# Self-attention exponentials turned by VectorE and DMAs instead of TensorE, with heads scored in pairs

## Chip, cores and metric

One of the eight cores of a Trainium2 chip runs the whole program. The metric is the device time of one execution, in microseconds; the kernel before takes 2255.77 us (median of three runs).

## The reference

A trunk of two layers is applied with the same weights to a prompt of 1024 rows and a sample of 256 rows, 1024 wide. Each layer adds to x the normalised projection of four groups of heads (attention, fourier, spatial gating, memory attention). Only the attention group is touched:

```python
q = apply_axial_rope(rms_norm(aq, q_g), cos, sin)      # 8 heads of 64
k = apply_axial_rope(rms_norm(ak, k_g), cos, sin)      # 2 heads of 64
s = jnp.einsum('bqkgd,bskd->bkgqs', qblk, k) * scale   # blocks of 128 queries
p = jax.nn.softmax(s, axis=-1)
o_att = jnp.einsum('bkgqs,bskd->bqkgd', p, v) * silu(ag)
```

The prompt's queries see 1024 keys, the sample's 256. All is in float32.

## The kernel before

The program is written as Python generators on top of a layer that assigns buffers and semaphores. Within a layer it runs the spatial gating, fourier and memory groups, then `attention_qkv` (keys, values and queries), `attention_gates`, `attention` and `output`. From the second step of `attention` on, the order of TensorE's instructions is the order in which they are written; on the other engines and on SP, which issues every DMA, the layer's scheduler sets the order.

`attention` walks over ten tiles of 128 queries (eight of the prompt, two of the sample), and in a tile over eight heads. Three stages are interleaved:

- `score` (L742): the head's scores, two matmuls of 512 keys for each half of a float32 product (the queries hold a high and a low part in rows 0 to 63 and 64 to 127, the keys' two parts are `kT[..][0]` and `kT[..][1]`), into a two-bank PSUM tile of the tag `s2` (two buffers). VectorE takes the row maximum (L755), ScalarE the exponentials and their sum (L757).
- `turn` (L760): the 128x1024 exponentials are transposed on TensorE in eight 128x128 pieces (L770) and copied out of PSUM by ScalarE (L773) and VectorE (L775), into a buffer `pt` with the keys on the partitions.
- `norm_gate` and `values` (L777, L788): while the next tile is scored, the last tile's `pt` is multiplied with the values, one block of 128 keys per head step, the two key heads into the upper and lower 64 rows of one PSUM bank; the result is multiplied with the gate over the row sum (L801) and stored (L803).

One step of the loop is written as: score of the next head, a step of the last tile's values, turn of this head. In tile 0 the last products of `attention_gates` are interleaved (L1012), in tiles 8 and 9 a product of `output` per head (L1014).

The tag `a16` has four buffers, which hold the layer's input `hT` until the gates are done and `pt` afterwards; `a8` has two, which hold the third group of `hT` until the last gate product.

Of the kernel before, what the change touches and what calls it, by code (L numbers as in the profile page):

```python
# [9 lines left out]
F32 = mybir.dt.float32  # L10
# [5 lines left out]
P = 128  # L16
# [58 lines left out]
def trunk_kernel(  # L75
# [93 lines left out]

# [1 line left out]
    slabs = []  # L171
# [26 lines left out]

# [1 line left out]
    def norm_begin(x_sb):  # L200
# [74 lines left out]

# [1 line left out]
    mk_d = [dram(f"mk{l}", [P, 4, 512]) for l in range(DEPTH)]  # L277
# [56 lines left out]

# [1 line left out]
    def sgu_pair(l, hT, i, o_d, wsT, bsp, vg, between=lambda: None):  # L336
# [43 lines left out]

# [1 line left out]
    def fourier_setup(l):  # L382
# [19 lines left out]
    def fourier_group(l, hT, h, o_d, cw, pos):  # L402
# [135 lines left out]

# [1 line left out]
    def memory_setup(l):  # L540
# [77 lines left out]

# [1 line left out]
    def attention_gates(l, hT, ag):  # L620
# [90 lines left out]

    def attention(l, q_d, kT, v8, v2, ag, o_d):
        def prep_q(t):
            q = c2([P, 8, HD])
            nc.sync.dma_start(q, q_d[t])
            qhl = c4([P, 8, 2, HD], F32R)
            split(qhl[:, :, 0, :], qhl[:, :, 1, :], q)
            return qhl

        def turn_q(qhl, qT, kvs):  # L720
            for kv in kvs:
                pt = mm([P, 4, P], F32R)
                for j in range(4):
                    nc.tensor.transpose(pt[:, j, :], qhl[:, 4 * kv + j].rearrange("p a d -> p (a d)"), ident_r)
                if kv == 0:
                    nc.scalar.copy(qT[:, 0:4], fv(pt))  # L726
                else:
                    nc.vector.tensor_copy(qT[:, 4:8], fv(pt))

        tiles = {}  # L730

        def open_tile(t):
            g, _ = group_of(t)
            nk = SEQ if g < 2 else DEC
            gt = c2([P, 4, P])
            nc.sync.dma_start(gt, ag[t])
            alloc = a16 if g < 2 else c4
            tiles[t].update(
                nk=nk, gt=gt, rs=st([P, 4, 2], tag="rowsum", bufs=3),
                pt=[alloc([P, nk // P, 4, P], F32) for _ in range(2)])  # L740

        def score(t, h):  # L742
            g, _ = group_of(t)
            e = tiles[t]
            nk = e["nk"]
            kv, j = h // 4, h % 4
            s = s2([P, 1024])
            for kg in ((0, 1) if g < 2 else (2,)):
                n = GROUPS[kg][1]
                c0 = GROUPS[kg][0] if g < 2 else 0  # L750
                for b in range(2):
                    nc.tensor.matmul(s[:, c0:c0 + n], e["qT"][:, h, :], kT[kg][b][:, kv, :],  # L752
                                     start=b == 0, stop=b == 1)
            nm = st([P, 1])
            nc.vector.tensor_reduce(nm, s[:, :nk], axis=AX.X, op=ALU.max, negate=True)  # L755
            p = c4([P, 1024])
            nc.scalar.activation(p[:, :nk], s[:, :nk], AF.Exp, bias=nm, accum_out=e["rs"][:, j, kv:kv + 1])  # L757
            e[h] = p

        def turn(t, h):  # L760
            e = tiles[t]
            nkt = e["nk"] // P
            kv, j = h // 4, h % 4
            p = e.pop(h)
            for half in range((nkt + 3) // 4):
                kn = min(4, nkt)
                pt = mm([P, 4, P])
                for kk in range(kn):
                    c0 = (half * 4 + kk) * P
                    nc.tensor.transpose(pt[:, kk, :], p[:, c0:c0 + P], ident)  # L770
                dst = e["pt"][kv][:, half * 4:half * 4 + kn, j, :]
                if half == 0:
                    nc.scalar.copy(dst, pt[:, :kn])  # L773
                else:
                    nc.vector.tensor_copy(dst, pt[:, :kn])  # L775

        def norm_gate(t):  # L777
            e = tiles[t]
            r = st([P, 4, 2], tag="rowsum_r", bufs=2)
            nc.vector.reciprocal(r, e["rs"])  # L780
            rb = c2([P, 4, 2, HD])
            nc.vector.tensor_copy(rb, r.unsqueeze(3).to_broadcast([P, 4, 2, HD]))
            rt = mm([P, 4, P])
            for j in range(4):
# [3 lines left out]
        def values(t, kt):  # L788
            e = tiles[t]
            nkt = e["nk"] // P  # L790
            if kt == 0:
                e["acc"] = mm([P, 4, P])
            acc = e["acc"]
            for kv in range(2):
                vt = (v8 if t < 8 else v2)[:, kt, kv * HD:(kv + 1) * HD]
                nc.tensor.matmul(acc[kv * HD:(kv + 1) * HD].rearrange("p j t -> p (j t)"), vt,  # L796
                                 e["pt"][kv][:, kt].rearrange("p j t -> p (j t)"),
                                 start=kt == 0, stop=kt == nkt - 1)
            if kt == nkt - 1:
                o = c2([P, 4, P])  # L800
                nc.vector.tensor_tensor(o, acc, e["gt"], ALU.mult)  # L801
                for j in range(4):
                    nc.sync.dma_start(o_d[j][:, t * P:(t + 1) * P], o[:, j, :])  # L803
                del tiles[t]

        qhl = prep_q(0)
        yield
        tiles[0] = dict(qT=c4([P, 8, P], F32R))
        turn_q(qhl, tiles[0]["qT"], (0, 1))
        open_tile(0)  # L810
        score(0, 0)
        yield
        work = [(t, h) for t in range(NT) for h in range(8)]
        todo = []
        for i, (t, h) in enumerate(work):
            if h == 2 and t + 1 < NT:
                qhl = prep_q(t + 1)
            if h == 4 and t + 1 < NT:
                tiles[t + 1] = dict(qT=c4([P, 8, P], F32R))
                open_tile(t + 1)  # L820
            if i + 1 < len(work):
                score(*work[i + 1])
            if todo:
                todo.pop(0)()
            if h in (4, 5) and t + 1 < NT:
                turn_q(qhl, tiles[t + 1]["qT"], (h - 4,))
            turn(t, h)
            if h == 7:
                for f in todo:
                    f()  # L830
                todo = [lambda t=t: norm_gate(t)]
                nkt = tiles[t]["nk"] // P
                todo += [lambda t=t, kt=kt: values(t, kt) for kt in range(nkt)]
                if nkt == 8:
                    a, b = todo[0], todo[1]
                    todo[0:2] = [lambda a=a, b=b: (a(), b())]
            yield t, h
        for f in todo:
            f()
        yield NT, 0  # L840

# [1 line left out]
    def rows_of(arr, t):  # L843
# [100 lines left out]

# [1 line left out]
    xin = [rows_of((x_prompt, x_sample), t) for t in range(NT)]  # L946
# [23 lines left out]
    for l in range(DEPTH):  # L970
# [136 lines left out]
```

## Time and profile before

| | us |
|---|---|
| median of three runs (2255.02 to 2256.5) | 2255.77 |
| span of the profiled execution | 2254.6 |
| TensorE busy in it | 2208.9 |
| VectorE busy | 1167.4 |
| ScalarE busy | 844.2 |
| GpSimd busy | 206.3 |

The page gives the profiled execution's span, from its first to its last instruction, and no time beside it; the span lies 1.2 us under the median of the runs. Busy matmul time is modelled, and two matmuls in the pipeline overlap, so a step's length is read from the distance of starts and not from the busy time.

### The profile page before, as it was taken

The numbers are of one execution on the slowest core, as the hardware profiler recorded it, in microseconds if no ns is written. First come the engines' busy times: TensorE is split into PE (matmuls) and PEld (weight loads), VectorE is DVE, ScalarE is ACT, GpSimd is POOL, SyncE is SP. The second block draws the span as 40 slices with busy tenths as digits, with TensorE's granted clock in tenths as the row PEclk, the third lists the DMA queues.
The fourth block names the chain that finished last, engine by engine and source line by source line (L and its number), as shares of the span: only waits on it lengthen the run. The fifth ranks groups of instructions, "written<-read, shape, count | busy, mean of one in ns | idle before, by whom it ended". The sixth has DMA issues, their size and how long they took to land.

```text
span 2254.6 us, 32607 instructions
## 1 busy us (share of the span) xinstructions
PE 2208.9 (98%) x12872; PEld 1837.5 (82%) x12872; DVE 1167.4 (52%) x2096; ACT 844.2 (37%) x1915; POOL 206.3 (9%) x376
## 2 busy tenths in 40 slices
PE   7999999999999999999999999999999999999997
PEld 7898988888998655578888988888899865567885
DVE  5345344545573777634465344445467377753445
ACT  6133332334332655541254222234342255554121
POOL 2010000000140000000062000000014000000005
PEclk9999999999999999999999999999999999999998
DMA  4123321201122210222343121020112221123234
GB/s 171 59 96 132 128 93 59 99 31 55 58 76 75 66 34 29 84 80 92 112 142 109 57 75 59 33 99 31 59 54 81 78 64 29 31 83 99 88 109 140
DMA packets 96200, 177.31 MB, mean 79 GB/s; under 512 B 12208, under 2 KB 47408, under 8 KB 96048
## 3 DMA queue, kind: packets, MB, share of 16 engines
q1 hardware_dynamic: 96048, 175.23, 23.1%
q8 instruction: 101, 1.65, 0.3%
q14 instruction: 51, 0.42, 0.1%
HBM read 129.05 MB, written 46.14 MB: 78 GB/s over the span
## 4 chain that ended last, share of the span: by engine, by line
PE 90%; ACT 2%; DMA 2%; DVE 2%; POOL 2%; issue 1%; SPq 0%; DVEq 0%; POOLq 0%; ACTq 0%
PE mm L248 34%; PE mm L877 16%; PE mm L261 12%; PE mm L796 6%; PE mm L770 6%; PE s L752 5%; PE mm L311 2%; PE mm L327 1%; PE s L422 1%; PE s L408 1%; PE s L576 1%; PE mm L609 1%; POOL c L902 1%; PE s L217 1%; DMA wr<-in_w_in_dram 1%
## 5 line engine op out<-in xcount | busy, mean ns | idle before, releaser
L248 PE MATMUL mm<-a,ws 128*128 128x512 f32 (+1 forms) x4032 | 795.4, 355 | 0.0
L248 PEld LDWEIGHTS mm<-a,ws 128*128 128x128 f32 x4032 | 663.9, 189 | 102.3 <-issue 0.5
L877 PE MATMUL mm<-ws,a 128*128 128x512 f32 x1632 | 380.5, 391 | 0.0
L877 PEld LDWEIGHTS mm<-ws,a 128*128 128x128 f32 x1632 | 303.9, 188 | 63.7 <-issue 1.6
L261 PE MATMUL mm<-ws,a 128*128 128x256 f32 x2400 | 302.7, 287 | 0.0
L261 PEld LDWEIGHTS mm<-ws,a 128*128 128x128 f32 x2400 | 295.6, 194 | 0.5 <-DVE a L234 0.2
L757 ACT ACTIVATE c<-s,st 128x1024 f32<-128x1024 f32 (+1 forms) x160 | 158.1, 988 | 154.8 <-DVE st L755 153.9
L755 DVE TENSOR_REDUCE st<-s 128x1 f32<-128x1024 f32 (+1 forms) x160 | 170.2, 1064 | 73.1 <-PE s L752 71.0
L770 PEld LDWEIGHTS mm<-ident,c 128*128 128x128 f32 x1088 | 117.1, 141 | 90.1 <-issue 26.0
L273 ACT ACTIVATE c<-mm 128x512 f32<-128x512 f32 (+1 forms) x96 | 50.7, 528 | 342.1 <-PE mm L248 338.3
L274 DVE SCALAR_TENSOR_TENSOR c<-c,mm 128x512 f32<-128x512 f32 (+1 forms) x96 | 57.3, 597 | 231.3 <-ACT c L273 231.3
L752 PE MATMUL s<-c,c 128*128 128x512 f32 (+1 forms) x576 | 162.6, 399 | 1.1 <-ACT c L726 1.1
L770 PE MATMUL mm<-ident,c 128*128 128x128 f32 x1088 | 151.8, 279 | 5.0 <-ACT c L757 5.0
L796 PE MATMUL mm<-a,c 128*64 128x512 f32 x512 | 140.2, 618 | 2.7 <-ACT a L773 2.7
L902 POOL TENSOR_TENSOR c<-c,c 128x512 f32<-128x512 f32 x40 | 56.1, 1401 | 891.5 <-ACT c L897 891.4
L166 ACT ACTIVATE ws<-wr,pre_g 128x256 fp32r<-128x256 f32 x304 | 126.6, 505 | 22.6 <-DMA wr<-in_w_in_dram 16.5
L167 DVE SCALAR_TENSOR_TENSOR ws<-wr,pre_g,ws 128x256 fp32r<-128x256 f32 x304 | 128.7, 484 | 2.2 <-ACT ws L166 2.0
L886 DVE TENSOR_TENSOR c<-c,mm 128x512 f32<-128x512 f32 x120 | 81.1, 682 | 85.1 <-PE mm L877 85.1
L775 DVE COPY a<-mm 128x512 f32<-128x512 f32 x128 | 88.3, 690 | 66.3 <-PE mm L770 66.1
L752 PEld LDWEIGHTS s<-c,c 128*128 128x128 f32 x576 | 98.5, 189 | 14.9 <-ACT c L726 1.3
L150 POOL TENSOR_TENSOR st<-st,mhalf 128x1 f32<-128x1 f32 (+3 forms) x120 | 99.7, 831 | 9.9
L148 POOL TENSOR_SCALAR st<-st 128x1 f32<-128x1 f32 (+3 forms) x120 | 27.2, 227 | 744.2 <-DVE st L654 455.5
(119 smaller groups left out, 2133.9 us busy)
## 6 DMA issues: line engine op xcount, KB each, us to landing
wr<-in_w_in_dram SPq DMA_DIRECT2D x76, 512.0 KB, 4.0
wr<-in_w_out_dram SPq DMA_DIRECT2D x32, 512.0 KB, 4.5
wr<-o SPq DMA_DIRECT2D x64, 256.0 KB, 2.9
c<-in_x_prompt_dram SPq DMA_DIRECT2D x16, 512.0 KB, 6.1
o<-c SPq DMA_DIRECT2D x32, 256.0 KB, 2.0
wr<-in_w_mem_kv_dram SPq DMA_DIRECT2D x16, 512.0 KB, 4.4
q<-c SPq DMA_DIRECT2D x40, 128.0 KB, 1.7
ag<-c SPq DMA_DIRECT2D x80, 64.0 KB, 1.6
```

The source lines that it names most:

```text
L150: nc.gpsimd.tensor_tensor(r, m, mhalf[:, :n], ALU.pow)
L166: nc.scalar.activation(w[:, 0, kk], raw[:, k], AF.Copy, scale=g)
L167: nc.vector.scalar_tensor_tensor(w[:, 1, kk], raw[:, k], g, fv(w)[:, 0, kk], ALU.mult, ALU.subtract)
L248: nc.tensor.matmul(acc[:, :n], w[:, a, k, c * P:(c + 1) * P], hT.t[g][b][:, k, :], start=i == 0, stop=i == 3 * KC - 1)
L261: nc.tensor.matmul(acc[:, :256], hT.t[g][a][:, k, tt * P:(tt + 1) * P], w[:, b, k, :], start=i == 0, stop=i == 3 * KC - 1)
L752: nc.tensor.matmul(s[:, c0:c0 + n], e["qT"][:, h, :], kT[kg][b][:, kv, :], start=b == 0, stop=b == 1)
L755: nc.vector.tensor_reduce(nm, s[:, :nk], axis=AX.X, op=ALU.max, negate=True)
L757: nc.scalar.activation(p[:, :nk], s[:, :nk], AF.Exp, bias=nm, accum_out=e["rs"][:, j, kv:kv + 1])
L770: nc.tensor.transpose(pt[:, kk, :], p[:, c0:c0 + P], ident)
L775: nc.vector.tensor_copy(dst, pt[:, :kn])
L796: nc.tensor.matmul(acc[kv * HD:(kv + 1) * HD].rearrange("p j t -> p (j t)"), vt, e["pt"][kv][:, kt].rearrange("p j t -> p (j t)"), start=k ...
L877: nc.tensor.matmul(acc, oT[g][c][:, a, tt * P:(tt + 1) * P], w[:, b, c, :], start=j == 0, stop=j == 11)
```

## The change

Heads are scored in pairs (a unit is a tile, a half of its heads and a key head; four units make a tile). The high part of the keys is multiplied as before. Of the low part, which needs 64 rows only, the first head of a pair uses rows 0 to 63 of the array and the second rows 64 to 127; `prep_q` lays the parts of odd heads the other way round for that. The exponentials no longer go to TensorE: VectorE transposes them in 32x32 blocks into a buffer `d` of the tag `a8` (1 MB per unit), one DMA stores `d` to DRAM, and four DMAs read it back, each into 32 partitions of `pt`. The values of a half tile are written two units after its second unit, in 256-column matmuls. The subtraction of the queries' low part and the spread of 1/sum go from VectorE to GpSimd. `output` is stepped twice per unit.

```diff
         def prep_q(t):
...
-            split(qhl[:, :, 0, :], qhl[:, :, 1, :], q)
+            for odd in range(2):
+                hi, lo = qhl[:, odd::2, odd, :], qhl[:, odd::2, 1 - odd, :]
+                nc.scalar.copy(hi, q[:, odd::2])
+                nc.gpsimd.tensor_tensor(lo, q[:, odd::2], fv(hi), ALU.subtract)
...
+        def open_half(t, hf):
+            e = tiles[t]
+            gt = c2([P, 2, P])
+            nc.sync.dma_start(gt, ag[t][:, 2 * hf:2 * hf + 2])
+            e[hf] = dict(gt=gt, rs=st([P, 2, 2], tag="rowsum", bufs=4), pt=a16([P, 2, 2 * e["nk"]], F32))
...
-            s = s2([P, 1024])
-            for kg in ((0, 1) if g < 2 else (2,)):
...
+            for s, h in zip(ss, hs):
+                for kg in kgs:
+                    nc.tensor.matmul(s[:, cols(kg)], e["qT"][:, h, :], kT[kg][0][:, kv, :], start=True, stop=False)
+            for kg in kgs:
+                for i, (s, h) in enumerate(zip(ss, hs)):
+                    r = slice(64 * i, 64 * i + 64)
+                    nc.tensor.matmul(s[:, cols(kg)], e["qT"][r, h, :], kT[kg][1][r, kv, :], start=False, stop=True)
...
-                    nc.tensor.transpose(pt[:, kk, :], p[:, c0:c0 + P], ident)
...
+            d = a8([P, 2 * nk], F32)
+            dv = d.rearrange("p (b k j q) -> p b k j q", b=4, j=2, q=32)
+            for j, p in enumerate(e.pop((hf, kv))):
+                nc.vector.transpose(dv[:, :, :, j].rearrange("p b k q -> p k b q"),
+                                    p[:, :nk].rearrange("p (k b q) -> p k b q", b=4, q=32))
+            n = nk // 2
+            far = dram(uid(f"turned{l}_"), [4, 32, 4, n])
+            nc.sync.dma_start(far.rearrange("a i b f -> (a i) (b f)"), d)
+            pt = e[hf]["pt"][:, kv].rearrange("p (a f) -> p a f", a=4)
+            for b in range(4):
+                nc.sync.dma_start(pt[32 * b:32 * b + 32], far[:, :, b].rearrange("a i f -> i a f"))
...
+            nc.gpsimd.tensor_copy(rb, r.unsqueeze(3).to_broadcast([P, 2, 2, HD]))
...
+                pt = e["pt"][:, kv].rearrange("p (a k f) -> p a k f", a=4, k=nkt)[:, :, kt]
+                nc.tensor.matmul(acc[kv * HD:(kv + 1) * HD].rearrange("p a j q -> p a (j q)"), vt, pt,
...
+        units = [(t, hf, kv) for t in range(NT) for hf in range(2) for kv in range(2)]
...
+        lag = 3
+        for i, (t, hf, kv) in enumerate(units):
...
+            if i + 1 < len(units):
+                if kv == 1:
+                    open_half(*units[i + 1][:2])
+                score(*units[i + 1])
...
+            turn(t, hf, kv)
+            if i >= lag and (i - lag) % 2 == 0:
...
+                todo.append([lambda u=(tt, hh): norm_gate(*u)] + steps[:nkt // 2])
+                todo.append(steps[nkt // 2:])
...
                 if t >= 8:
                     next(out)
+                    next(out)
```

How it moves instructions, at three places. On SP before, between two tiles of the prompt (`ag` and `q` are loads of gates and queries, `o` the stores of a tile's result):

```order
L715 DMA c_1109_7911<-q_4_5916 128x512
L736 DMA c_1122_7963<-ag_4_6769 128x512
L803 DMA o_0_177<-c_1092_7836 128x128
L803 DMA o_1_178<-c_1092_7836 128x128
L803 DMA o_2_179<-c_1092_7836 128x128
L803 DMA o_3_180<-c_1092_7836 128x128
L715 DMA c_1163_8135<-q_5_5917 128x512
```

On SP now, over some two units (L782 is the store of `d`, L785 x4 its four reads into `pt`, here a):

```order
L785 DMA a_1185_8103<-turned_1208_8182 32x4x512 x4
L782 DMA turned_1220_8225<-a_1219_8222 128x2048
L782 DMA turned_1234_8276<-a_1233_8273 128x2048
L741 DMA c_1236_8294<-ag_6_6771 128x256
L785 DMA a_1185_8103<-turned_1220_8225 32x4x512 x4
L815 DMA o_2_179<-c_1235_8290 128x128
L815 DMA o_3_180<-c_1235_8290 128x128
L785 DMA a_1212_8203<-turned_1234_8276 32x4x512 x4
L782 DMA turned_1247_8325<-a_1246_8322 128x2048
```

Where a whole tile had six DMAs, each unit now adds a store and four reads, and the store of the next unit can stand ahead of the reads of this one. On VectorE, at the start of the first layer's attention (L766 is the row maximum, L274 a gate product's last step, L778 the block transposes into `d`):

```order
L274 SCALAR_TENSOR_TENSOR c_958_7255<-c_958_7255,mm_7230 128x256
L766 TENSOR_REDUCE st_7271<-s_960_7261 128x1
L766 TENSOR_REDUCE st_7275<-s_961_7262 128x1
L778 STREAM_TRANSPOSE a_942_7160<-c_929_7099 128x8x4x32
L778 STREAM_TRANSPOSE a_942_7160<-c_931_7103 128x8x4x32
L778 STREAM_TRANSPOSE a_955_7221<-c_939_7154 128x8x4x32
L778 STREAM_TRANSPOSE a_955_7221<-c_941_7158 128x8x4x32
```

The first unit's blocks are turned only after the fourth unit's maxima, because `d` lies in buffers that the gates still read. On TensorE now, two units of the steady state (L758 high part, L762 the 64-row matmuls, L795 gate over sum, L807 values):

```order
L758 MATMUL s_1254_8355<-c_693_5346,c_1225_8248 128x512
L758 MATMUL s_1254_8355<-c_695_5348,c_1225_8248 128x512
L758 MATMUL s_1255_8356<-c_693_5346,c_1225_8248 128x512
L758 MATMUL s_1255_8356<-c_695_5348,c_1225_8248 128x512
L762 MATMUL s_1254_8355<-c_694_5347,c_1225_8248 128x512
L762 MATMUL s_1255_8356<-c_694_5347,c_1225_8248 128x512
L762 MATMUL s_1254_8355<-c_696_5349,c_1225_8248 128x512
L762 MATMUL s_1255_8356<-c_696_5349,c_1225_8248 128x512
L807 MATMUL mm_8339<-a_1185_8103,c_698_5351 64x256 x8
```

Eight 128-row transposes per head are gone from between the scores and the values; the values wait for the reads into `pt`.

## Rows read from the trace of the kernel before

**Rows 1.** The page: busy time, share of the span and instructions
```profile
PE 2208.9 (98%) x12872; PEld 1837.5 (82%) x12872; DVE 1167.4 (52%) x2096; ACT 844.2 (37%) x1915; POOL 206.3 (9%) x376
...
PE 90%; ACT 2%; DMA 2%; DVE 2%; POOL 2%; issue 1%; SPq 0%; DVEq 0%; POOLq 0%; ACTq 0%
```
**Rows 2.** Windows over one prompt tile: stretch, busy us of each engine, PEclk, DMA share, GB/s
```profile
808.00:833.00 25.00, 25.00 (x142) 14.92 (x141) 18.34 (x24) 14.64 (x27) 0.00 (x0) 1.00 0.11 32
```
**Rows 3.** Timeline of TensorE in that tile: start, us, line, tiles, count
```profile
808.73 0.60 PE L785 MATMUL mm<-ident,c 128*128 128x128 f32 x4
809.26 1.08 PE L796 MATMUL mm<-a,c 128*64 128x512 f32 x4
...
811.12 1.17 PE L752 MATMUL s<-c,c 128*128 128x512 f32 x4
812.23 1.08 PE L796 MATMUL mm<-a,c 128*64 128x512 f32 x4
813.24 1.09 PE L770 MATMUL mm<-ident,c 128*128 128x128 f32 x8
814.08 1.17 PE L752 MATMUL s<-c,c 128*128 128x512 f32 x4
...
833.55 0.60 PE L785 MATMUL mm<-ident,c 128*128 128x128 f32 x4
```
**Rows 4.** Timeline of VectorE and ScalarE there, idle time ahead in brackets
```profile
815.30 1.22 DVE L755 TENSOR_REDUCE st<-s 128x1 f32<-128x1024 f32 x1 [0.24 <-PE s L752]
...
816.61 1.12 ACT L757 ACTIVATE c<-s,st 128x1024 f32<-128x1024 f32 x1 [0.77 <-DVE st L755]
```
**Rows 5.** Groups by form: line, operation, count, busy us and mean ns, idle before
```profile
L755 DVE TENSOR_REDUCE st<-s 128x1 f32<-128x1024 f32 x128 | 156.7, 1224 | 31.5 <-PE s L752 29.5
L144 DVE TENSOR_TENSOR c<-c,c 128x1024 fp32r<-128x1024 f32 x8 | 9.8, 1226 | 9.6 <-ACT c L143 9.6
L209 DVE TENSOR_SCALAR c<-c,st 128x1024 f32<-128x1024 f32 x10 | 7.5, 752 | 9.0 <-POOL st L150 7.3 <-ACT a L233 1.5
L662 DVE TENSOR_TENSOR c<-mm,c 128x128 f32<-128x128 f32 x80 | 19.2, 281 | 0.0
```
**Rows 6.** DMA issues: tiles, count, KB each, median us from issue to landing
```profile
c<-q SPq DMA_DIRECT2D x20, 256.0 KB, 2.7
o<-c SPq DMA_DIRECT2D x80, 64.0 KB, 1.6
o<-c SPq DMA_DIRECT2D x8, 512.0 KB, 2.6
```
**Rows 7.** Windows at the program's start, loads queued behind each other
```profile
9.00:19.00 10.00, 7.00 (x30) 6.38 (x31) 7.30 (x15) 9.53 (x19) 1.70 (x4) 1.00 1.03 412
```
**Rows 8.** Timeline of TensorE, start of attention in the first layer
```profile
727.23 1.20 PE L752 MATMUL s<-c,c 128*128 128x512 f32 x4 [0.52 <-ACT c L726]
728.26 3.02 PE L248 MATMUL mm<-a,ws 128*128 128x256 f32 x24
731.12 1.09 PE L752 MATMUL s<-c,c 128*128 128x512 f32 x4
```
**Rows 9.** Timeline of TensorE where the sample's tiles begin
```profile
931.10 0.48 PE L752 MATMUL s<-c,c 128*128 128x256 f32 x2
...
934.55 1.07 PE L796 MATMUL mm<-a,c 128*64 128x512 f32 x2 [1.36 <-ACT a L773]
935.55 0.44 PE L770 MATMUL mm<-ident,c 128*128 128x128 f32 x2
935.75 3.00 PE L877 MATMUL mm<-ws,a 128*128 128x512 f32 x12
938.59 0.40 PE L752 MATMUL s<-c,c 128*128 128x256 f32 x2
```
**Rows 10.** TensorE's last matmuls (timeline), and the windows behind them
```profile
2214.48 24.98 PE L877 MATMUL mm<-ws,c 128*128 128x512 f32 x108
...
2240.00:2250.00 10.00, 0.00 (x0) 0.00 (x0) 7.50 (x9) 1.45 (x4) 8.60 (x13) 0.59 0.35 131
```

More of the change, by code (lines that the diff above doesn't have):

```diff
@@ L733, in open_tile, with score @@
             g, _ = group_of(t)
[L734 to L742, printed above, removed]
+            tiles[t] = dict(nk=SEQ if g < 2 else DEC, qT=c4([P, 8, P], F32R))
+        def open_half(t, hf):
[3 more added lines that the diff above has]
+            e[hf] = dict(gt=gt, rs=st([P, 2, 2], tag="rowsum", bufs=4), pt=a16([P, 2, 2 * e["nk"]], F32))
+        def score(t, hf, kv):
             g, _ = group_of(t)
@@ L780, in norm_gate @@
+        def norm_gate(t, hf):
+            e = tiles[t][hf]
+            r = st([P, 2, 2], tag="rowsum_r", bufs=2)
             nc.vector.reciprocal(r, e["rs"])
[L781 to L784, printed above, removed]
+            rb = c2([P, 2, 2, HD])
+            nc.gpsimd.tensor_copy(rb, r.unsqueeze(3).to_broadcast([P, 2, 2, HD]))
+            rt = mm([P, 2, P])
+            for j in range(2):
@@ L799, in values @@
             if kt == nkt - 1:
[L800 to L804, printed above, removed]
+                o = c2([P, 2, P])
+                nc.vector.tensor_tensor(
+                    o.rearrange("p j (a q) -> p j a q", a=4), acc.rearrange("p a j q -> p j a q"),
+                    e["gt"].rearrange("p j (a q) -> p j a q", a=4), ALU.mult)
@@ L806, in attention @@
+                for j in range(2):
+                    nc.sync.dma_start(o_d[2 * hf + j][:, t * P:(t + 1) * P], o[:, j, :])
+        units = [(t, hf, kv) for t in range(NT) for hf in range(2) for kv in range(2)]
         qhl = prep_q(0)
         yield
-        tiles[0] = dict(qT=c4([P, 8, P], F32R))
-        turn_q(qhl, tiles[0]["qT"], (0, 1))
         open_tile(0)
-        score(0, 0)
+        for kv in range(2):
+            turn_q(qhl, tiles[0]["qT"], kv)
+        open_half(0, 0)
+        score(*units[0])
@@ L812, in attention @@
         yield
-        work = [(t, h) for t in range(NT) for h in range(8)]
         todo = []
-        for i, (t, h) in enumerate(work):
-            if h == 2 and t + 1 < NT:
+        lag = 3
+        for i, (t, hf, kv) in enumerate(units):
+            if i % 4 == 0 and t + 1 < NT:
                 qhl = prep_q(t + 1)
-            if h == 4 and t + 1 < NT:
-                tiles[t + 1] = dict(qT=c4([P, 8, P], F32R))
+            if i % 4 == 2 and t + 1 < NT:
                 open_tile(t + 1)
-            if i + 1 < len(work):
-                score(*work[i + 1])
-            if todo:
[L824 to L829, printed above, removed]
-                    f()
[L831 to L837, printed above, removed]
@@ L838, in attention @@
-        for f in todo:
-            f()
+            if i + 1 < len(units):
+                if kv == 1:
+                    open_half(*units[i + 1][:2])
+                score(*units[i + 1])
+            if i % 4 >= 2 and t + 1 < NT:
+                turn_q(qhl, tiles[t + 1]["qT"], i % 4 - 2)
+            turn(t, hf, kv)
+            if i >= lag and (i - lag) % 2 == 0:
+                tt, hh, _ = units[i - lag]
+                nkt = tiles[tt]["nk"] // P
+                steps = [lambda u=(tt, hh), kt=kt: values(*u, kt) for kt in range(nkt)]
+                todo.append([lambda u=(tt, hh): norm_gate(*u)] + steps[:nkt // 2])
+                todo.append(steps[nkt // 2:])
@@ L840, in attention @@
+            if todo:
+                for f in todo.pop(0):
+                    f()
+            yield t, 2 * (i % 4)
+        last = [u for u in range(0, len(units), 2) if u + lag >= len(units)]
+        for f in (f for g in todo for f in g):
+            f()
+        for u in last:
+            tt, hh, _ = units[u]
+            norm_gate(tt, hh)
+            for kt in range(tiles[tt]["nk"] // P):
+                values(tt, hh, kt)
         yield NT, 0
```

66 lines of the change are left out of this document (24 added, 42 removed).

## The prediction

> **What bounds the kernel now.** I read the page's busy shares and the chain of waits first [rows 1]: TensorE is busy for 98% of the span and carries 90% of the chain, VectorE is at 52%. So the question is what the attention stage costs TensorE, and who takes over when it costs less. The window over one prompt tile [rows 2] says the same of that stage: TensorE 25.0 of 25 us, VectorE 18.3, ScalarE 14.6, the DMA engines 0.11 of their time at 32 GB/s.
>
> TensorE's timeline [rows 3] gives the prices. From one gate step (L785) to the next is a tile: 833.55 - 808.73 = 24.8 us for eight heads, so 6.2 us for two. A head is score, values, transposes, and the next score follows 2.96 us later: 1.11 us for the four score matmuls, 1.01 for one step of values, 0.84 for the eight transposes. The rest of a tile is the gate step and the turned queries.
>
> I forecast the pace of one **unit** (two heads) in each prompt tile, which must be compared with 6.2 us. There are 32 such units in a layer. The new pace is that of the slowest of TensorE, VectorE with its chain, and the DMA engines.
>
> **TensorE, per unit.** The transposes go: 2 x 0.84 = 1.7 us. The scores were eight matmuls of about 0.25 us; now four, and four 64-row ones that count as two if they run side by side: 1.5 us, or 2.0 if they don't. That two matmuls into different parts of the array do overlap is shown for columns: the values' 64-column matmuls of the two key heads, four entries of about 0.6 us busy each, take 1.01 us together [rows 3]. For rows nothing is shown; I take 1.5. The values keep their columns (twice the matmuls, half as wide), 2.0 us; the gate step and the queries add about 0.3. Sum 3.8 us, upper end 4.3. Alone this would be 2.4 us per unit less.
>
> **VectorE, per unit.** Two row maxima of 1.22 us stay [rows 5]. The copies out of PSUM go, and two block transposes of 128x1024 come. No row shows one. The nearest is a 128x1024 subtraction in SBUF, 1.23 us; the fastest operation of that size takes 0.75; eight separate 128x128 operations would take 8 x 0.28 = 2.25, my upper end. I take 1.22. Small steps (a reciprocal and two half-width products per half tile) add about 0.5. Sum 2 x 1.22 + 2 x 1.22 + 0.5 = 5.4 us; ends 4.5 and 7.5. The chain through the two score tiles is no longer than that: 0.24 us from the scores to the maxima, 2.44 for both, 1.1 for the second exponential [rows 4], 1.1 for the second head's scores, 4.9 in all. GpSimd's four small operations per tile stand beside 25 us of an engine that was idle there [rows 2], so I cost them at nothing; were they late, SP's load of the next gates would wait for them, and the reads queued behind it.
>
> **The DMA engines, per unit.** A unit now stores 128 x 2048 x 4 bytes = 1.05 MB and reads as much back; the old traffic, 32 GB/s over a tile, is 0.2 MB per unit. When loads stand behind each other the engines move 412 GB/s at a share of 1.03 [rows 7]. At that rate the store takes 2.55 us and the old traffic 0.5. The store spreads over all partitions as those loads do, and the landing times of stores (0.46 MB more in 1.0 us) bear the rate out [rows 6].
>
> The reads are the term on which the sum turns. There are four, of 0.26 MB in runs of 2 KB, each into 32 partitions only. Lower end: the 412 GB/s, 0.64 us each, 2.55 in all. Upper end: each waits out the one before, 2.7 us as the load of queries with the same bytes and run length [rows 6], 10.8 in all; that I exclude, since SP issues the four in a row and loads overlap [rows 7]. Nearest is that load of queries without its fixed part: a 64 KB store lands after 1.6 us, 0.15 of which are bytes, so 2.7 - 1.5 = **1.2 us** each, 4.8 in all. I take that and not the 412 GB/s, because every load behind that figure wrote to 128 partitions at once and a quarter read doesn't.
>
> The Trainium skill speaks against this change here: its page SBUF — State Buffer, section "Door 1: The DMA port swizzle", says that a transfer into 32 partitions reaches 8 of 16 ports, and that a second transfer beside it does not help. From its 218 GB/s one would estimate 4.8 us for the four reads, which gives the forecast below, where the rate of rows 7 gives the first rival. No transfer in this trace goes to fewer than 128 partitions, so no row shows it.
>
> Sum: 2.55 + 4.8 + 0.5 = **7.85 us** per unit. That is over VectorE's 5.4 and TensorE's 3.8, so the DMA engines set the pace, and it is 1.65 us over the 6.2 of before. TensorE's and VectorE's savings are then hidden; TensorE waits in front of the values.
>
> I looked for queues that would make it worse. On SP the store of a unit waits for VectorE, and the next reads stand behind it; so do a half tile's result stores, which wait for values on TensorE. But while the reads of one unit are awaited, the reads and stores of the next are already with the engines (4.8 + 2.55 us of work), so no gap has to open.
>
> **Start and end of the stage.** The first store can't leave early: `d` lies in buffers that the last gate product reads, and VectorE's order puts the first block transposes behind the fourth unit's maxima. The first scores start at 727.2 [rows 8] and take 1.6 us; three more follow one chain apart, 728.8 + 3 x 4.9 = 743.5; maxima to 746.2; stores leave at 748.6 and 751.1. Both stores are through at 753.7, both units' reads at 753.7 + 9.6 = 763.3, landed 1.5 later: 765. Each of the other 15 halves adds 2 x 7.85: the last prompt half lands at 765 + 235.5 = 1000.
>
> Before, the corresponding point is 931.1, the score of the sample's second head [rows 9]. What TensorE has left behind that point is shorter now. Before, beside 20 products of `output` and more: 10.0 us of values, gate and a wait of 1.4 for the prompt's last tile, 5.0 for 15 scores (0.33 each), 2.9 for 16 heads' transposes, 5.6 for the sample's queries and values, 23.5 in all. Now: 4.3 for the last half, 5.0 for five pairs, 5.6, so 14.9; and two products (2 x 2.7) are already done while the last half is awaited. That is 14 us less. The layer ends 1000 - 14 - 931 = 55 us later. Both layers: 110. Against the profiled span, 2254.6 + 110 = 2365; the median stands 1.2 above the span: **2366 us**.
>
> **Rivals.**
>
> A, *the reads run at the full rate* (the other sign). At 412 GB/s a unit costs the DMA engines 2.55 + 2.55 + 0.5 = 5.6, VectorE 5.4: the last half lands at 760 + 30 x 5.6 = 928, the layer ends 928 - 14 - 931 = 17 us earlier, 2222 us in all. It decides at 6.2 us per unit, so the four reads must stay under about 3.1 us in sum (0.8 each). For it: the measured 412 GB/s. Against: quarters, and no reserve, since the engines would be full without a gap.
>
> B, *block transposes are slow*. With A's reads and 2.25 us per transpose, VectorE needs 7.5 per unit: the last half at 985, 40 us later per layer, 2336. With the forecast's reads it costs nothing, the DMA engines stay slower.
>
> C, *TensorE at half its clock*. Behind the program's last matmul, with TensorE idle, the granted clock averages 0.59 over ten us [rows 10]. In the forecast TensorE waits about half of the time; at half clock its 3.8 us become 7.6, still under 7.85, so it costs a few us at the stage's end at most. With A's reads it would set the pace at 7.6: 2342. Against: in the tiles of before gaps of up to 1.4 us [rows 9] left the clock at full, and A's gaps are of that size. The Trainium skill, TensorE: Matmul & The Clock Gate, section "HAM oscillation", has matmul groups that wait for data again and again run at the lower clock; by that rule C goes with any pace that DMAs set.
>
> D, *the 64-row matmuls don't run side by side*: 4.3 us per unit on TensorE, hidden in the forecast, the same 2366.
>
> **How the numbers follow.** Forecast (with D) 0.62; A 0.20; B 0.06; C 0.06; something worse in the queues 0.06. The forecast's own range takes 1.0 to 1.35 us per read: 7.05 to 8.45 per unit, 2315 to 2405. To leave out no more than 2 in 10 the range must reach B and C and half of A: 2220 to 2410. About 0.2% (4.5 us) can be told from no change. Faster: most of A, 0.17. Same: where A's pace comes out near 6.2, 0.04. Slower: 0.79.
>
> **What would show it.** Right: over a prompt tile the DMA share near 1 with under 320 GB/s, TensorE under two thirds busy and idle in front of the values (L807) until a read into `pt` lands, quarter reads landing after well over 2.7 us, units 7 to 8.5 us apart. A: 400 GB/s and units 5.6 apart. B: block transposes (L778) of 2 us and VectorE without idle time. D: the four L762 matmuls starting 0.2 us apart one by one instead of in twos. The forecast is wrong if the units' distance is under 6.2 us, or if something other than a read releases the values.

## The result, and the profile after

The changed kernel takes **2405.64 us** (median, 2400.43 to 2409.44) against 2255.39 beside it: 1.0668 times as long, 95% interval 1.0647 to 1.0689. That is 150 us more, where the forecast had 110 (2366, range 2220 to 2410). Its profiled execution has a span of 2407.3 us.

The page of the changed kernel: TensorE and VectorE with their share of the span, then the slices (granted clock, DMA share, GB/s), one group, and two rows of DMA issues with the median us to landing.

```profile
PE 2175.7 (90%) x12328; PEld 1786.5 (74%) x12328; DVE 1204.8 (50%) x2128; ACT 778.6 (32%) x1795; POOL 249.6 (10%) x456
...
PEclk9999999999998777799999999999999887879998
DMA  4123411212126999952342121121222799995233
GB/s 170 62 94 132 156 49 58 86 36 71 64 72 199 279 263 288 260 182 80 113 163 74 49 81 47 57 86 36 70 69 73 212 278 263 285 255 173 80 122 131
...
L807 PE MATMUL mm<-a,c 128*64 128x256 f32 x1088 | 202.8, 475 | 120.6 <-DMA a<-turned 116.6
...
turned<-a SPq DMA_DIRECT2D x64, 1024.0 KB, 9.0
a<-turned SPq DMA_DIRECT2D x256, 256.0 KB, 7.1
```

TensorE fell from 98% to 90% busy [rows 1], and 116.6 us of its idle time stand in front of the values (L807) until a read of the turned exponentials lands. Where attention runs, the DMA share is at 9 with 255 to 288 GB/s, and the granted clock, which is 0.50 or 1.00 in most of the 2 us windows below, has a mean of 0.7 in a slice.

Windows of the changed kernel, columns as in [rows 2]:

```profile
760.00:780.00 20.00, 11.30 (x50) 5.75 (x50) 7.58 (x9) 2.34 (x4) 0.00 (x0) 0.66 1.01 281
780.00:800.00 20.00, 11.97 (x60) 6.46 (x58) 10.76 (x12) 5.33 (x10) 0.40 (x1) 0.76 1.05 282
800.00:820.00 20.00, 9.94 (x56) 5.01 (x56) 14.07 (x16) 8.12 (x15) 2.17 (x4) 0.84 1.01 282
820.00:840.00 20.00, 16.66 (x74) 9.06 (x74) 10.08 (x11) 6.44 (x12) 1.41 (x2) 0.67 1.06 254
```

And its DMA traffic from 760 to 1000 us, the last figure the share of the engines' time:

```profile
DMA packets 27569, 66.19 MB, mean 276 GB/s; under 512 B 3061, under 2 KB 8181, under 8 KB 23845
...
q1 hardware_dynamic: 27557, 66.04, 99.9%
```

The DMA engines are full over the whole stage, at 276 GB/s, where the loads of [rows 7] had 412 at about the same share. TensorE, busy for all of the tile in [rows 2], is busy for 163.8 of these 240 us, 0.68; that counts matmuls that run longer at the lowered clock, and in the first three windows above it is 0.50 to 0.60. TensorE's timeline, with the first scores of the second layer, and then those of the kernel before:

```profile
726.34 1.20 PE L758 MATMUL s<-c,c 128*128 128x512 f32 x4 [0.52 <-ACT c L730]
727.46 0.73 PE L762 MATMUL s<-c,c 64*128 64x512 f32 x4
728.12 3.14 PE L248 MATMUL mm<-a,ws 128*128 128x256 f32 x24
...
768.65 3.64 PE L807 MATMUL mm<-a,c 128*64 128x256 f32 x14 [3.82 <-DMA a<-turned]
...
774.57 1.95 PE L807 MATMUL mm<-a,c 128*64 128x256 f32 x16
...
786.88 3.65 PE L807 MATMUL mm<-a,c 128*64 128x256 f32 x14 [6.16 <-DMA a<-turned]
...
1003.49 3.65 PE L807 MATMUL mm<-a,c 128*64 128x256 f32 x14 [3.32 <-DMA a<-turned]
...
1866.51 1.19 PE L758 MATMUL s<-c,c 128*128 128x512 f32 x4 [0.52 <-ACT c L730]
```
```profile
1791.45 1.20 PE L752 MATMUL s<-c,c 128*128 128x512 f32 x4 [0.53 <-ACT c L726]
```

The values of nearly every half tile start when its last read lands. The first half lands at 768.65, the fifteenth at 1003.49: 28 units in 234.84 us, **8.39 us per unit** against the forecast's 7.85 and the 6.2 of before. Fourteen matmuls behind such a wait take 3.55 to 3.67 us in 13 of these 15 halves (1.91 in two); sixteen behind other work mostly take 1.95.

Two windows with stores at the front of the queue and two with quarter reads, in the changed kernel:

```profile
752.00:754.00 2.00, 0.00 (x0) 0.00 (x0) 2.00 (x5) 0.14 (x1) 0.00 (x0) 0.75 0.97 397
754.00:756.00 2.00, 0.00 (x0) 0.00 (x0) 2.00 (x3) 2.00 (x3) 0.00 (x0) 0.50 0.97 395
...
762.00:764.00 2.00, 0.25 (x1) 0.28 (x2) 0.00 (x0) 0.00 (x0) 0.00 (x0) 0.50 1.06 219
764.00:766.00 2.00, 0.83 (x2) 0.01 (x1) 0.00 (x0) 0.00 (x0) 0.00 (x0) 0.50 1.07 213
```

A store into DRAM from all 128 partitions runs at 396 GB/s, quarter reads at 216, with the engines full in both.

### The profile page after: what moved, and what is told of

Its sections match the earlier page's. It is cut to its first block, busy times and chain, and to the rows that moved or that the text cites. A ratio compares the mean times of both kernels' runs of the same rounds, so it can differ in the third digit from the quotient of the medians.

```text
span 2407.3 us, 32425 instructions
## 1 busy us (share of the span) xinstructions
PE 2175.7 (90%) x12328; PEld 1786.5 (74%) x12328; DVE 1204.8 (50%) x2128; ACT 778.6 (32%) x1795; POOL 249.6 (10%) x456
## 5 line engine op out<-in xcount | busy, mean ns | idle before, releaser
L807 PE MATMUL mm<-a,c 128*64 128x256 f32 x1088 | 202.8, 475 | 120.6 <-DMA a<-turned 116.6
L766 DVE TENSOR_REDUCE st<-s 128x1 f32<-128x1024 f32 (+1 forms) x160 | 162.7, 1058 | 206.9 <-PE s L762 206.2
L807 PEld LDWEIGHTS mm<-a,c 128*64 128x64 f32 x1088 | 98.3, 166 | 198.1 <-issue 160.4
L778 DVE STREAM_TRANSPOSE a<-c 128x1024 f32<-128x1024 f32 (+1 forms) x160 | 164.5, 1063 | 54.9 <-DMA turned<-a 29.8
L274 DVE SCALAR_TENSOR_TENSOR c<-c,mm 128x512 f32<-128x512 f32 (+1 forms) x96 | 57.1, 597 | 230.8 <-ACT c L273 230.8
L758 PE MATMUL s<-c,c 128*128 128x512 f32 (+1 forms) x288 | 104.7, 478 | 66.3 <-ACT c L768 36.7
L758 PEld LDWEIGHTS s<-c,c 128*128 128x128 f32 x288 | 56.7, 225 | 116.0 <-ACT c L768 54.0
L144 DVE TENSOR_TENSOR ws<-wr,ws 128x1024 fp32r<-128x1024 f32 x48 | 57.0, 1222 | 59.1 <-ACT ws L143 59.1
```

Of the source, the lines that this page charges most:

```text
L758: nc.tensor.matmul(s[:, cols(kg)], e["qT"][:, h, :], kT[kg][0][:, kv, :], start=True, stop=False)
L778: nc.vector.transpose(dv[:, :, :, j].rearrange("p b k q -> p k b q"), p[:, :nk].rearrange("p (k b q) -> p k b q", b=4, q=32))
L807: nc.tensor.matmul(acc[kv * HD:(kv + 1) * HD].rearrange("p a j q -> p a (j q)"), vt, pt, start=kt == 0, stop=kt == nkt - 1)
```

## The experiments

**The reads into every fourth partition.** Same bytes, count and run length; only the partitions of a quarter change, with the key columns permuted to fit.

```diff
...
-                nc.sync.dma_start(pt[32 * b:32 * b + 32], far[:, :, b].rearrange("a i f -> i a f"))
+                nc.sync.dma_start(pt[b::4], far[:, :, b].rearrange("a i f -> i a f"))
```

> The four reads of a unit go to every fourth partition of pt (partitions b, b+4, ...), not to 32 neighbouring ones; the keys' columns are permuted to fit. Bytes, runs of 2 KB and number of DMAs stay. Theory (32 neighbouring partitions take a transfer in at half rate): the reads go at about 400 GB/s, a unit costs the DMA engines 5.6 us instead of 8.4, the pace is 5.5 to 6.0 us per unit, the time 2215 to 2250 us. Rival (the number of small transfers, or stores and reads in a mix, cost the rate): nothing changes, 2395 to 2415 us.

Measured: 2331.97 us, 1.0349 [1.0325, 1.0373]. Half of the loss goes, half stays, so neither number holds. The first and the fifteenth half of this run:

```profile
767.78 3.65 PE L808 MATMUL mm<-a,c 128*64 128x256 f32 x14 [2.33 <-DMA a<-turned]
...
976.26 3.65 PE L808 MATMUL mm<-a,c 128*64 128x256 f32 x14 [1.94 <-DMA a<-turned]
```

Units are 7.45 us apart. The partitions are a cause, and something else is left.

**Only the first unit stored.** One store for each shape and layer; every read fetches that one. This leaves out the other stores, and with them the waits for a store to land before its reads; the result is not the attention's.

```diff
...
-            far = dram(uid(f"turned{l}_"), [4, 32, 4, n])
-            nc.sync.dma_start(far.rearrange("a i b f -> (a i) (b f)"), d)
+            if n not in once:
+                once[n] = dram(uid(f"turned{l}_"), [4, 32, 4, n])
+                nc.sync.dma_start(once[n].rearrange("a i b f -> (a i) (b f)"), d)
+            far = once[n]
```

> Only the first unit of each shape and layer is stored; every unit's reads fetch that one, so 1.05 MB per unit of stores is left out and the attention's result is that of other exponentials. Theory (reads at half rate): the reads alone need 4.8 to 5.4 us per unit, so with the old traffic the DMA engines stay busy for 0.9 or more of the time at 230 GB/s or less, pace 5.4 to 5.9, time 2215 to 2255 us. Rival (mix of stores and reads): the reads go at 400 GB/s once alone, the DMA share falls to 0.6 at a pace of VectorE's 5.4, 2210 to 2220 us.

Measured: 2261.73 us, 1.0034 [1.0023, 1.0045], some 7 us over the theory's range. Windows of reads alone, last columns clock, DMA share, GB/s:

```profile
764.00:766.00 2.00, 1.51 (x8) 1.06 (x10) 0.00 (x0) 0.00 (x0) 0.00 (x0) 0.50 1.07 211
...
778.00:780.00 2.00, 1.42 (x6) 0.63 (x6) 2.00 (x3) 1.26 (x4) 0.00 (x0) 1.00 1.07 209
```

Quarter reads by themselves fill the DMA engines at 209 GB/s: 0.26 MB takes 1.25 us, 5.0 us per unit (the forecast: 1.2 and 4.8). The stores, their bytes and the waits for them together, are the other large part: without them the time falls by 144 us. Past the first half, TensorE no longer waits for reads: three gate steps stand at 827.12, 848.89 and 870.65, so a tile takes 21.8 us, 5.4 per unit, with VectorE busy for 18.7 of 20 us (860 to 880). The theory's pace is met, but reads and VectorE come to about the same here, and this run doesn't tell which of them sets it. Then there is one late load of queries in each layer, without which the time would lie below the theory's upper end. In the first layer it is this cast on ScalarE, and then the scores that wait for it on TensorE:

```profile
808.47 0.71 ACT L722 CAST c<-c 128x256 fp32r<-128x256 f32 x2 [17.67 <-DMA c<-q]
```
```profile
810.34 2.32 PE L759 MATMUL s<-c,c 128*128 128x512 f32 x4 [15.86 <-ACT c L769]
```

**Both together: spread reads, one store.**

> e1_spread and e2_one_store together: reads into every fourth partition, and only the first unit of each shape and layer is stored; all reads fetch that one, so the attention outputs are those of other heads. Measures the reads' rate by itself. Theory (reads spread over the partitions run at the rate of the loads, 412 GB/s): DMA share under 0.7, no wait of TensorE for reads, units set by TensorE and its partners at 5.2 to 5.6 us, 2215 to 2245 us. Rival (the spread reads have a limit of their own at about 300 GB/s): DMA share over 0.8 with under 330 GB/s, 2245 to 2262 us.

Measured: 2222.6 us, 0.9851 [0.9834, 0.9867], in the theory's range. It differs from the run before only in where the reads land, and that is worth 39 us. Nearly all of that is the late load, which is gone: from the first scores of one layer to those of the next it is 1048.4 us, 17.9 less than in the run before, with the same steady tile. Windows of the reads, one of the steady state, and two scores a tile apart:

```profile
768.00:770.00 2.00, 2.00 (x14) 1.05 (x14) 0.41 (x1) 0.00 (x0) 0.00 (x0) 1.00 1.04 362
770.00:772.00 2.00, 1.43 (x14) 0.69 (x10) 2.00 (x3) 1.09 (x2) 0.00 (x0) 1.00 1.04 379
...
840.00:860.00 20.00, 16.21 (x106) 8.71 (x106) 18.57 (x22) 10.22 (x19) 2.17 (x4) 1.00 0.80 243
```
```profile
806.45 1.20 PE L760 MATMUL s<-c,c 128*128 128x512 f32 x4 [1.87 <-ACT c L731]
...
827.94 1.23 PE L760 MATMUL s<-c,c 128*128 128x512 f32 x4 [1.88 <-ACT c L731]
```

Spread reads run at some 370 GB/s, 1.8 times the rate, and not at the 412 of the theory; the DMA share is 0.76 from 800 to 900 us, between theory and rival. TensorE waits for no read there. The tile is 21.5 us, 5.4 per unit, with VectorE busy for 0.92 of the time: this is what the rest of the changed kernel allows as it stands, some 33 us under the kernel before. The 1.87 us that TensorE waits in each tile for the queries' copy are still in it.

**Quarters in the order 0, 2, 1, 3**, so that neighbours in the queue go to different halves of the partitions.

```diff
-            for b in range(4):
+            for b in (0, 2, 1, 3):
```

> The changed kernel with the four quarter reads of a unit issued in the order 0, 2, 1, 3, so that neighbours in the queue go to partitions 0 to 31 and 64 to 95, then 32 to 63 and 96 to 127. Theory (a read into 32 neighbouring partitions is slow by itself, and the queue's order lets no second one help it): within 10 us of the changed kernel, 2395 to 2415 us. Rival (two reads in flight into different halves share the load): reads at 300 GB/s or more together, units near 7 us, 2310 to 2350 us.

Measured: 2368.72 us, 1.0503 [1.0487, 1.0518]; between the two. Two halves of this run:

```profile
766.28 3.64 PE L807 MATMUL mm<-a,c 128*64 128x256 f32 x14 [3.44 <-DMA a<-turned]
...
983.37 3.58 PE L807 MATMUL mm<-a,c 128*64 128x256 f32 x14 [2.12 <-DMA a<-turned]
```

28 units in 217.09 us, 7.75 each, 0.64 less than in the changed kernel; 60 such units in two layers make 38 us, and 37 were measured. So the order alone is worth about an eighth of the reads' 5.0 us, and the expectation that it would change nothing was wrong.

**Full-row matmuls in place of the 64-row ones.**

```diff
...
-                    r = slice(64 * i, 64 * i + 64)
+                    r = slice(0, P)
```

> The change, with the low part of the keys multiplied over all 128 rows again (four full matmuls for four 64-row ones), the rest as changed. Theory (DMA engines set the pace): 0.4 us more per unit on TensorE is hidden, 2400 to 2412 us. Rival (TensorE at a lowered clock sets the pace): 64 x 0.4 to 0.9 us more, 2430 to 2460 us.

Measured: 2394.33 us, 1.062 [1.0597, 1.0642]: more TensorE work, and 11 us less, under both numbers. It ran twice (2392.83 and 2395.82), and the changed kernel's four runs lie 9 us apart, the lowest at 2400.43. Units are 8.26 us apart, 0.13 less, 8 us in 60 units. The mean granted clock was 0.955 against 0.942. The pairs of 64 rows bring nothing here; why more work is a little faster isn't settled.

**Pairs on TensorE.** Pairs and lag kept, but eight transposes a head as before, no DMAs.

```diff
...
-            d = a8([P, 2 * nk], F32)
...
+                    for kk in range(kn):
+                        nc.tensor.transpose(ps_t[:, kk, :], p[:, c0:c0 + P], ident)
+                    if half == 0:
+                        nc.scalar.copy(out, src)
+                    else:
+                        nc.vector.tensor_copy(out, src)
```

> The pairs and the two-unit lag of the change stay, the block transposes, the store and the reads are undone: TensorE transposes the exponentials in 128x128 pieces as before, ScalarE and VectorE copy them out of PSUM. Theory: TensorE 1.5 + 1.7 + 2.0 + 0.3 = 5.5 us per unit against 6.2 before, no DMA in the way, 64 x 0.7 = 40 us under the kernel before: 2200 to 2235 us. Rival (64-row matmuls gain nothing, or the two score tiles of a pair make a longer chain): 2250 us or more.

Measured: 2275.18 us, 1.009 [1.0073, 1.0107], the rival. Its timeline of TensorE:

```profile
821.75 1.95 PE L810 MATMUL mm<-a,c 128*64 128x256 f32 x16 [0.93 <-DVE a L788]
823.63 1.19 PE L758 MATMUL s<-c,c 128*128 128x512 f32 x4
824.75 0.73 PE L762 MATMUL s<-c,c 64*128 64x512 f32 x4
825.41 0.54 PE L729 MATMUL mm<-ident_r,c 128*128 128x128 f32 x4
```

A pair of scores costs 1.12 + 0.66 = 1.78 us, not the 1.5 of the forecast (before: 2 x 1.11); and more than it saves goes into waits, most of them for VectorE's copies out of PSUM, up to 0.9 us at a time, which single heads did not have in their tile [rows 3]. The tile from 806.64 to 833.16 us takes 26.5, against 24.8 before; 2.5 of it are such waits.

**Queries a tile earlier, reads spread.** In the first experiment ScalarE stood before its cast of the queries for 48 us, and the exponentials behind it. Its waits between 740 and 1000 us (us in total, times, longest):

```profile
ACT c L723 <- DMA c<-q: 48.4, 6, 10.6
```

```diff
...
             if i % 4 == 0 and t + 1 < NT:
                 qhl = prep_q(t + 1)
+                if t + 2 < NT:
+                    load_q(t + 2)
...
```

> The reads as in e1_spread (every fourth partition), and the queries of a tile are loaded one tile earlier. In e1_spread ScalarE stood 48 us of the 260 us from 740 to 1000 before the cast of the queries (L723) because their load stood behind reads in SP's queue, and the exponentials stood behind that cast. Theory (this wait is what keeps e1_spread from the 5.6 us per unit of full-rate transfers): the wait falls under 5 us, units 6.2 us or less apart, 2250 to 2275 us. Rival (SP issues stores and reads in order and each waits for a buffer, so store, read and values of the units follow each other whatever the queries do): units stay near 7.4 us, 2315 to 2335 us.

Measured: 2331.82 us, 1.0334 [1.0319, 1.035]; the rival's number. The wait is gone and the time is the same. Two windows, and SP's longest wait between 740 and 980 us:

```profile
780.00:800.00 20.00, 16.14 (x90) 8.74 (x92) 12.12 (x14) 6.33 (x12) 2.22 (x4) 0.83 0.94 332
840.00:860.00 20.00, 16.53 (x93) 9.09 (x90) 12.86 (x14) 7.86 (x15) 1.82 (x3) 0.87 0.89 319
```
```profile
SPq L791 <- DMA turned<-a: 47.0, 15, 7.5
```

The DMA engines are at 0.92 (760 to 960 us) with 323 GB/s, and units are 7.23 us apart: the transfers alone keep the engines busy for 0.92 x 7.23 = 6.7 us, more than the 6.2 of before. The rest are gaps, and for 47.0 us SP had to wait for a store to land before it could issue the reads behind it, as the rival has it; no run parts the bytes from this order. The late queries did not cost time here. Stores alone reach 396 and spread reads 370; why the mixture gets 323 is open.

**Half of the units on TensorE**, and the same with early queries.

```diff
...
         def turn(t, hf, kv):
+            if kv == 1:
+                return turn_pe(t, hf, kv)
...
```

> The changed kernel, but only the first key head's pair of each half tile goes through DMAs; the second pair is turned on TensorE and copied out by ScalarE and VectorE as in e4_pairs_pe. Two units then cost the DMA engines one store and four reads, 2.55 + 5.2 + 1.0 = 8.8 us, and TensorE two units of 3.8 and one set of transposes of 1.8, 9.4 us, against 12.4 before. Theory (the transfers' rate was the bound, halving them frees it): units 5.0 to 5.7 us apart, TensorE over 85% busy in the stage at full clock, 2210 to 2245 us. Rival (the orders of the pairs and of SP's queue cost more than the transfers): units over 6.2 us, 2260 us or more, as in e4_pairs_pe.

> e7_hybrid with the queries loaded one tile earlier. Theory (the late load of the queries is a second wait, which the transfers of half the units already cause): 5 to 20 us under e7_hybrid. Rival (with half the transfers the queries land in time): within 4 us of e7_hybrid.

Measured: 2282.88 us, 1.0128 [1.0107, 1.0148], and 2284.13 us, 1.0122 [1.0106, 1.0139]: the rivals, both. The DMA share is about 0.7, and the transfers no longer hold anything in a tile. TensorE of the second run:

```profile
787.04 1.19 PE L763 MATMUL s<-c,c 128*128 128x512 f32 x4 [1.80 <-ACT c L735]
...
791.94 1.95 PE L832 MATMUL mm<-a,c 128*64 128x256 f32 x16 [0.59 <-DVE a L793]
...
798.29 0.73 PE L763 MATMUL s<-c,c 128*128 128x512 f32 x2 [0.74 <-ACT c L773]
...
811.81 1.19 PE L763 MATMUL s<-c,c 128*128 128x512 f32 x4 [1.88 <-ACT c L735]
```

This tile is 24.8 us, as before, and the next ones 25.2 to 26.3: the 3.4 us of transposes saved came back as waits for ScalarE and VectorE, 13.0 us in the 80 from 780 to 860.

**Queries turned a unit earlier, first tile on TensorE.** The edit against the last run:

```diff
...
-            if kv == 1:
+            if kv == 1 or t == 0:
...
-            if i % 4 == 2 and t + 1 < NT:
+            if i % 4 == 1 and t + 1 < NT:
                 open_tile(t + 1)
...
-            if i % 4 >= 2 and t + 1 < NT:
-                turn_q(qhl, tiles[t + 1]["qT"], i % 4 - 2)
+            if i % 4 in (1, 2) and t + 1 < NT:
+                turn_q(qhl, tiles[t + 1]["qT"], i % 4 - 1)
```

> e8_hybrid_early_q with two waits taken out: the queries of the next tile are turned one unit earlier (TensorE waited 1.88 us in each tile for ScalarE's copy of them, 13.8 us per layer), and the first tile goes through TensorE alone (the first reads were awaited 7.6 us, and the values behind them ran 1.7 us longer at half clock). Theory (these waits were on the path): 13.8 + 9 us per layer less, 2284 - 46 = 2238 us, 2230 to 2255. Rival (ScalarE's order of exponentials and copies holds the units 6.2 us apart, and the wait only moves to the exponentials): 2270 to 2285 us.

Measured: 2255.22 us, 0.9998 [0.9989, 1.0008]: 29 us less, at the upper end of the theory, and the same as the kernel before. The wait for the queries' copy is gone, but the tile is still 24.2 us, because scores, gate step and values wait in its place:

```profile
788.53 0.73 PE L763 MATMUL s<-c,c 128*128 128x512 f32 x2 [0.73 <-ACT c L773]
...
794.19 0.41 PE L820 MATMUL mm<-ident,c 128*128 128x128 f32 x2 [0.86 <-DVE a L793]
...
806.40 1.95 PE L832 MATMUL mm<-a,c 128*64 128x256 f32 x16 [0.92 <-DVE a L793]
...
812.76 0.73 PE L763 MATMUL s<-c,c 128*128 128x512 f32 x2 [0.73 <-ACT c L773]
```

Five tiles take 121.2 us, and 127.1 in the run before. A layer, from its first scores to the next one's, got 13.5 shorter; how much of that each of the two edits brought, no run tells.

**Three of four units through DMAs, spread**, in two forms. In the first, the last run with its reads into every fourth partition, the block transposes pick every fourth column:

```diff
...
-            if kv == 1 or t == 0:
+            if (hf, kv) == (1, 1) or t == 0:
...
-                                    p[:, :nk].rearrange("p (k b q) -> p k b q", b=4, q=32))
+                                    p[:, :nk].rearrange("p (k q b) -> p k b q", b=4, q=32))
...
```

> e11_hybrid_early_turn with three of four units through DMAs, read into every fourth partition; the keys keep their order, the block transposes take every fourth column instead. TensorE's tile of 24.2 us loses one set of transposes (2.0) and the waits for VectorE's copies behind it (0.9): 21.3 us. The DMA engines move 3 x 2.1 + 0.8 = 7.1 MB per tile, at the 320 GB/s that e6_spread_early_q reached 22.2 us. Theory (transfers and TensorE balanced so, DMA engines just the slower): tiles 22 to 23 us apart over 15 halves each layer, 2230 to 2245 us. Rival (near its limit the queue's landings come in bursts and TensorE waits and loses its clock again, as in e6): tiles of 25 us or more, 2262 to 2290 us.

Measured: 2277.81 us, 1.0102 [1.0087, 1.0116]. The rival's number, by another mechanism: reads are seldom waited for (7.7 us in a layer), scores are (29.9). VectorE's block transposes between 760 and 920 us:

```profile
L803 DVE STREAM_TRANSPOSE a<-c 128x1024 f32<-128x1024 f32 x36 | 71.6, 2019 | 0.0
```

A block transpose of every fourth column takes 2.02 us. The second form keeps the columns together, permutes the keys as the first experiment did, and ScalarE writes the exponentials of TensorE's units with a step of four instead:

```diff
...
+                if (hf, kv) == (1, 1) or t == 0:
+                    pv = pv.rearrange("p (k i b) -> p k b i", i=32, b=4)
+                    sv = sv.rearrange("p (k b i) -> p k b i", i=32, b=4)
...
```

> e12_three_quarters with its slow part mended: there the block transposes of every fourth column took 2.02 us instead of 1.20, and VectorE was busy for 17.5 of 20 us. Now the keys are put in the order of e1_spread, the block transposes read neighbouring columns again, and ScalarE writes the exponentials of the units that TensorE turns with every fourth column, so that these come out in the order of the values. VectorE's tile loses 6 x 0.82 = 4.9 us. Theory (VectorE held e12_three_quarters at 25.3 to 26.4 us per tile): tiles of 21.5 to 23 us, TensorE's 21.3 being the floor, 2220 to 2245 us. Rival (the landings come in bursts near 0.8 of the DMA engines' time): tiles over 24 us, 2250 to 2275 us.

Measured: 2264.37 us, 1.0041 [1.0027, 1.0054]; the rival's number, but again not its mechanism, since TensorE waited for no read between 780 and 920 us. Tiles take 25 us (the transposes of two tiles start at 808.53 and 833.58). ScalarE's timeline there:

```profile
823.21 1.12 ACT L778 ACTIVATE c<-s,st 128x1024 f32<-128x1024 f32 x1
...
827.22 2.08 ACT L778 ACTIVATE c<-s,st 128x1024 f32<-128x1024 f32 x1 [0.26 <-DVE st L772]
...
829.15 2.07 ACT L778 ACTIVATE c<-s,st 128x1024 f32<-128x1024 f32 x1
```

The price moved along: 2.08 us for a spread write against 1.12, on the chain from score to score, where TensorE waits 1.15 and 1.19 us behind such a pair. The transposes that follow ran 3.68 us at a lowered clock at 833.58, 1.97 in the form before; the two prices weren't parted. No version here that computes the attention beats the kernel before.

## Why the prediction was right

**The bound.** The forecast that the DMA engines set the pace holds: a share of 0.999 over the stage at 276 GB/s, the values released by reads. Of its signs only "TensorE under two thirds busy" is missed, with 0.68. It is settled by the runs that take transfers or partitions away and leave TensorE's work alone: 144 us less without stores, 74 less with spread reads. In size it was less good: 110 us were forecast and 150 came. The 2405.64 lies 4 us within the stated range, and just past the 2405 that the forecast's own reads at their slowest would give, though the reads were not at their slowest.

**The mis-sized term.** The sum of 2.55 + 4.8 + 0.5 = 7.85 us came out as 8.39. The reads are 5.0 (1.25 each instead of 1.2), the store's rate of 396 GB/s makes 2.65; 8.15 in all. The other 0.24 is left over; stores and reads in a mixture are the likely place, but no run shows that price alone. Per layer 0.54 x 30 = 16 us, and the first half landed 3.7 later (768.65 for 765): 55 + 20 = 75. From the first scores of layer 0 (726.34, before 727.23) to those of layer 1 (1866.51, before 1791.45) the measured loss is 76. The 14 us less of TensorE's left-over work came about as forecast: from the values of the last prompt half (1020.15) to layer 1's scores it is 846.4 us, and before from 931.10 [rows 9] it is 860.4.

**The 1.2 us per read** were right by luck. They were worked out from a load into all 128 partitions, and nothing in that sum is about 32 of them; by it a spread read would take 1.2 us too, and at 370 GB/s it takes 0.7. Only the reason for leaving the 412 GB/s, that a quarter read doesn't write to all partitions, was the right one. (Unrounded, 2.7 - 1.45, the sum even gives the 1.25 that were measured.)

The Trainium skill (SBUF — State Buffer, "Door 1: The DMA port swizzle") gives about 218 GB/s for 32 neighbouring partitions; the 207 to 219 here agree with it, and the 370 of spread partitions with its port map. The prediction's remark on a second transfer belongs to the same page's section "Can I just issue two DMAs to hit both halves?". It has two transfers to different halves gain only some 6%; the order 0, 2, 1, 3 brought about an eighth here, and the measurement decides.

**Rival A** (2222 us) asked for all transfers at 412 GB/s. It needs more than other partitions: spread reads alone gave 2332, with stores and reads together at 308 to 323 GB/s. Its time, 2222.6, came only without the stores, and not by its mechanism: reads ran at 370 and the DMA engines were not full.

**Rival B** fell: block transposes take 1.22 us, as taken from the nearest operations [rows 5]. Its price appeared in the form with every fourth column, 2.02 us, near its bound of 2.25.

**Rival C** is there and hidden, as said: the clock was granted at 0.66 to 0.87 in the windows from 760 to 1000 us, values took 3.64 us in place of 1.95, and the reads were still slower. The Trainium skill's "HAM oscillation" (TensorE: Matmul & The Clock Gate) describes matmul groups that start at the lower clock again after each wait for data; the rows agree. Whether the lower clock cost a few us all the same is open, since the run with full rows had a higher one and was 11 us faster.

**Rival D** fell: four 64-row matmuls take 0.66 us, four full ones 1.12, so they do run side by side; at 773.91 us of the changed kernel the first two start within 0.1 us. But the pair's scores are 1.78 us, not 1.5: the full four cost 0.28 each, as the 1.11 us for four in [rows 3] already said, and not 0.25. Hidden here, it mattered on TensorE.

**The queues.** "No gap has to open" held: the engines were full. Others did wait behind them: VectorE's block transposes 29.8 us in the whole run for stores to free `d`, and ScalarE's cast of the queries 38 us in one layer, for a load behind the reads. Taking the second wait away was tried with spread reads, and changed nothing there.

**What the 2.4 us hid.** The 2.4 us per unit on TensorE were not to be had even without a DMA bound. The prediction's own term for VectorE, 5.4 us per unit, leaves 0.8 of them, and the best run without the bound (spread, one store) ran at just these 5.4, with VectorE busy for 0.92 of the time.

## What to carry to other kernels

Work that leaves a full engine must be priced on the engine that takes it, and for a DMA by the partitions of each transfer: the same bytes ran at 209 GB/s into 32 neighbouring partitions and at 370 into every fourth. A late load or a stalled copy beside a full DMA queue can be a mere sign (removed with spread reads, it changed nothing) or cost time by itself (17.7 us in a layer with one store): remove it alone before rebuilding around it. And where the rest of a chain, here score, maximum, exponential through two PSUM buffers and the copies beside it, is nearly as long as TensorE's work, time taken from TensorE returns as waits; half of the transposes gone left the tile at 24.2 us at best. More than two such buffers were not tried.

## What the runs showed of the hardware that was not expected

- Quarter reads in the order 0, 2, 1, 3 are faster than 0, 1, 2, 3: 7.75 us per unit against 8.39.
- A step of four fp32 elements makes an operation over 128x1024 1.7 to 1.9 times as long: block transposes 2.02 us against 1.22 on VectorE (reading), exponentials 2.08 against 1.12 on ScalarE (writing).
- More TensorE work made the kernel 11 us faster (full rows, 2394.33 in two runs against 2405.64 in four), at a mean clock of 0.955 against 0.942. Whether the clock is the reason was not tried.
